# FFN up products with the operand's high and low part side by side: one 512-column matmul for two of 256, pairs of PSUM banks, and TensorE in program order

## The chip, the cores and the metric

The kernel runs on one core of a Trainium2 chip. The metric is the time of one execution on the device, in microseconds, as the median of several runs. A core has five engines with queues of their own: TensorE (matmuls, PE in the profile; its weight loads are PEld), VectorE (DVE), ScalarE (ACT), GpSimd (POOL) and SyncE (SP, which here only issues loads). Matmuls read SBUF and write PSUM, which has eight banks of 512 fp32 columns in each of 128 partitions.

## The reference

One transformer block in fp32 on 512 tokens of width 1024: a gated FFN, a mixer (short convolution and gated linear attention), a second gated FFN, and a last norm.

```python
def swiglu(x, w_gu, w_down):
    g, u = jnp.split(x @ w_gu, 2, axis=-1)
    return (jax.nn.silu(g) * u) @ w_down

def reference(x, ...):
    for l in range(DEPTH):      # DEPTH = 1
        x = x + 0.5 * swiglu(rmsnorm(x, norm_ffn1_g[l]), ffn1_w_gu[l], ffn1_w_down[l])
        x = x + hybrid_mixer(rmsnorm(x, norm_mix_g[l]), ...)
        x = x + 0.5 * swiglu(rmsnorm(x, norm_ffn2_g[l]), ffn2_w_gu[l], ffn2_w_down[l])
    return rmsnorm(x, final_norm_g)
```

The change concerns the "up" products `x @ w_gu` of both FFNs (1024 by 2 x 2816).

## The kernel before, in words

**Precision.** An fp32 product is made from three matmuls in a reduced format (fp32r). Each operand is split into a high part, the rounded value, and a low part, what is left. For a weight these are `wh` (ScalarE, a cast, line 358) and `wl` (VectorE, a subtraction, line 359); for the activations ("op") they are made in `Operands.make` (lines 599 and 600). The product is wh times high + wh times low + wl times high.

**Sets of seven products.** Most of the up projection runs in sets. A set takes 256 columns of the gate g and 256 of u and computes them by a Strassen-like scheme on halves of the depth (1024) and of the tokens (512): seven products instead of eight, called m1, p2, q6, p5, q7, p4, p3, each with another sum of weight blocks and another sum of activation blocks of 256 tokens (HW). There are nine sets in each FFN; the first 512 columns of g and of u run as plain products (`mm_group`, `mm_single`) before them. The order of the products comes from `order`: q6, p5, q7 of set s, m1 of the next set, p4 of s, p2 of the next, p3 of s; so the next set's first products lie between the last ones of this set.

**One product** (`Set.run`) is four pieces of depth k, two halves e of 128 output columns, and three matmuls of 256 tokens each (line 551): 24 matmuls, all into one PSUM bank. The bank is "b" for m1, q6, q7, p4 (which accumulate in it one after the other), "a" for p2, "c" for p5 and p3. After m1, q6 and q7 the state of the bank is kept: ScalarE copies it to SBUF (line 556, tiles "tp"). `done` of `up_set` then makes g1 after p2 (line 715, silu 716), u2 after q7 (line 720), the first half of `hid` after p4 (line 724), g2 after p3 (line 729, silu 730) and the second half of `hid`. In the second FFN, `natural(i)` transposes one block of X (four small matmuls, line 817) after a set.

**Weights** (`Weights`): tiles "f" are loaded by SP, some sums of blocks are made by DMAs that accumulate (line 333, issued by GpSimd) and one by VectorE (line 343). `take` issues the cast and the split of weights two products ahead; `wh` and `wl` have three buffers each, so a cast waits until TensorE has used the buffer of three products before.

**Order.** A scheduler orders each engine's instructions when the program is built, by when they are ready in its own model, and in program order where several are ready; it draws up TensorE's queue as well. In a block of manual schedule an engine keeps program order. At run time every engine works through its queue in that order, and semaphores hold an instruction until what it reads is there and what it overwrites has been read.

**PSUM.** A pool `ps` of six single banks serves all matmuls with tile "mm" (taken in turn), a pool `pa` of two banks the rest ("aux": transposes, sums of squares, two of the down projection's eight banks).

Of the kernel before, what the change touches and what calls it, by code (L numbers as in the profile page):

```python
# [78 lines left out]
HW = 256  # L79
# [136 lines left out]
def block_kernel(ctx: ExitStack, tc: tile.TileContext, xT, vecs, gf, gup, wgl, wts, out):  # L216
    nc = tc.nc
# [2 lines left out]

    front = ctx.enter_context(tc.tile_pool(name="front", bufs=1))
    keep = ctx.enter_context(tc.tile_pool(name="keep", bufs=1))
    ps = ctx.enter_context(tc.tile_pool(name="ps", bufs=6, space=bass.MemoryType.PSUM))
    pa = ctx.enter_context(tc.tile_pool(name="pa", bufs=2, space=bass.MemoryType.PSUM))

    cnt = [0]

# [10 lines left out]
    def tile_of(pool, shape, dtype=F32):  # L238
        cnt[0] += 1
        return pools[pool].tile(shape, dtype, tag=pool, name=f"{pool}{cnt[0]}")  # L240

    def T(dtype=F32):
        return tile_of("tp", [P, S], dtype)

    def MM():
        cnt[0] += 1
        return ps.tile([P, S], F32, tag="mm", name=f"mm{cnt[0]}")

    def AUX():
        cnt[0] += 1  # L250
        return pa.tile([P, S], F32, tag="aux", name=f"aux{cnt[0]}")
# [23 lines left out]
    class Weights:  # L275
# [3 lines left out]
        def __init__(self, ahead):  # L279
            self.ahead = ahead  # L280
            self.issued = 0
            self.taken = 0
            self.end = 0
            self.ready = []
            self.raw = {}
            self.loads = {}
            self.sums = {}
            self.pre = {}
# [88 lines left out]
    W = Weights(2)  # L377
# [12 lines left out]
    def mm_single(mat, kt, col, ah, al):  # L390
        o = MM()
        for u in single(mat, kt, col):
            h, l = W.take(u)
            for i in range(u[2]):
                k = u[1] + i
                mm3(o, h[:, i * P : (i + 1) * P], l[:, i * P : (i + 1) * P],
                    ah[k], al[k], k == 0, k == kt - 1)
        return o

    def mm_group(mat, kt, cols, ah, al, extra=None, slow=False):  # L400
        o = [MM() for _ in cols]
        n = len(cols)
        for u in group(mat, kt, cols, slow):
            h, l = W.take(u)
            for i in range(u[2]):
                k = u[1] + i
                for j, (w, a) in enumerate(((h, ah), (h, al), (l, ah))):
                    for c in range(n):
                        s = (i * n + c) * P
                        nc.tensor.matmul(o[c], w[:, s : s + P], a[k], start=k == 0 and j == 0,  # L410
                                         stop=k == kt - 1 and j == 2)
                if extra is not None:
                    extra(k)
        return o
# [108 lines left out]
    def mul(out_, a, b, eng=None):  # L523
        (eng or nc.vector).tensor_tensor(out=out_, in0=a, in1=b, op=ALU.mult)


    class Set:
# [8 lines left out]

        def run(self, p):
            b = {"m1": "b", "p2": "a", "q6": "b", "p5": "c", "q7": "b", "p4": "b", "p3": "c"}[p]
            fresh = b not in self.bank
            if fresh:  # L540
                self.bank[b] = MM()
            o = self.bank[b]
            bh, bl = self.group.get(p)
            h, l = W.take()
            for k in range(4):
                for e in range(2):
                    s = slice(k * HW + e * P, k * HW + (e + 1) * P)
                    t = slice(k * HW, (k + 1) * HW)
                    to = o[:, e * HW : (e + 1) * HW]
                    for j, (ww, aa) in enumerate(((h, bh), (h, bl), (l, bh))):  # L550
                        nc.tensor.matmul(to, ww[:, s], aa[:, t],  # L551
                                         start=fresh and k == 0 and e == 0 and j == 0,
                                         stop=k == 3 and j == 2, skip_group_check=True)
            if p in self.keep:
                v = T()
                nc.scalar.copy(v, o)  # L556
                self.v[p] = v
            self.done(self, p)

    class Operands:  # L560

        ORDER = ("m1", "p2", "p5", "q6", "q7", "p3", "p4")

        def __init__(self, b):
            self.b = b
            self.parts = {}
            self.sums = set()

# [19 lines left out]
        def make(self, p):  # L590
            if p in self.parts:
                return
            i = self.ORDER.index(p)
            if i > 0:
                self.make(self.ORDER[i - 1])
            v = self.sum(p)
            h, l = (tile_of("op", [P, 1024], F32R) for _ in range(2))
            hv, lv = (t.rearrange("p (k t) -> p k t", t=HW) for t in (h, l))
            nc.scalar.copy(hv, v)  # L599
            nc.vector.tensor_tensor(out=lv, in0=v, in1=hv.bitcast(F32), op=ALU.subtract)  # L600
            self.parts[p] = (h, l)
# [31 lines left out]
    def run_sets(make, ahead=2, hooks={}, tall=None):  # L633


        at = W.taken
        seq = []
        while STEPS[at + len(seq)][1] is not None:
            seq.append(STEPS[at + len(seq)])
        sets = {n: None for n, _ in seq if n not in TALL}  # L640
        number = {n: i for i, n in enumerate(sets)}
        for n, i in number.items():
            sets[n] = make(i)
        for i, (n, p) in enumerate(seq):
# [12 lines left out]
    def ffn(up, down, norm, nxt, plain, at):  # L657
# [7 lines left out]
        o = mm_group(up, KD, (0, DFF, P, DFF + P), xh, xl, extra=finish, slow=nxt is not None)  # L665
# [17 lines left out]
                xn[j, l] = v  # L683
            return xn[j, l]

        xo = Operands(normed)

        def plain_pair(f, g, u):
            s, t = T(), T()
            mul(s, g, row)  # L690
            nc.scalar.activation(s, s, AF.Silu)
            mul(t, u, row)
            mul(hid[:, f], s, t)
# [5 lines left out]
        for f in range(2, plain):  # L699
# [5 lines left out]
                xo.sum("q6")  # L705
            plain_pair(f, g, u)

        def up_set(i):
            h = hid[:, plain + 2 * i : plain + 2 * i + 2]

            def done(s, p):
                bank, v = s.bank, s.v
                if p == "p2":
                    g1 = T()
                    nc.vector.tensor_tensor(out=g1, in0=bank["a"], in1=v["m1"], op=ALU.add)
                    nc.scalar.activation(g1, g1, AF.Silu)
                    s.g1 = g1
                if p == "q7":
                    u2 = T()
                    nc.vector.scalar_tensor_tensor(out=u2, in0=bank["c"], scalar=-1.0, in1=v["q7"],  # L720
                                                   op0=ALU.mult, op1=ALU.subtract)
                    s.u2 = u2
                if p == "p4":
                    nc.vector.scalar_tensor_tensor(
                        out=h[:, :, :HW], in0=pair(bank["b"]), scalar=-1.0, in1=pair(s.g1),
                        op0=ALU.mult, op1=ALU.mult)
                if p == "p3":
                    g2 = T()
                    nc.vector.tensor_tensor(out=g2, in0=bank["c"], in1=v["q6"], op=ALU.add)
                    nc.scalar.activation(g2, g2, AF.Silu)  # L730
                    mul(h[:, :, HW:], pair(s.u2), pair(g2))
                    if nxt is None and i < KD:
                        natural(i)

            return Set(xo, done)

        def pair(t):
            return t.rearrange("p (e t) -> p e t", t=HW)

        run_sets(up_set)  # L740

        def split_hid(k):

# [10 lines left out]
        def banks():  # L754
            return [AUX(), AUX()] + [MM() for _ in range(KD - 2)]
# [12 lines left out]
        o = banks()  # L768
        hls = {k: split_hid(k) for k in (CHUNK, CHUNK + 2)}
        more = [4, 6, 8, 10, "m1", "p2", "p5", "q6", "q7", "p3"]  # L770
        for k in range(CHUNK, KF - TAIL1):
# [3 lines left out]
            if more:  # L775
                n = more.pop(0)
# [25 lines left out]
        o = banks()  # L802
# [702 lines left out]
```

## Time and profile before

| | |
|---|---|
| runs | 1195.34, 1195.03, 1195.0 us; median 1195.03 |
| profiled execution | 1195.04 us, span 1193.3 us |
| mean granted TensorE clock | 0.998 |
| PE, PEld busy | 99%, 91% of the span |
| DVE, ACT, POOL busy | 71%, 50%, 9% |
| HBM | 124.55 MB read, 8.39 MB written |

A busy share is an average over the whole kernel. What a change in one stage is worth is read from the chain of waits: the chain that ended last is followed back from the last instruction, at each step to what released it. A group of instructions is given by line, engine, operation, output and inputs, count, then busy us, mean ns of one, and the idle time before it. In a timeline a row is start us, length us, engine, line and operation; in brackets the idle time before it and who ended it.

### The profile page before, as it was taken

How to read it: one execution, taken by the hardware profiler on the slowest of the kernel's cores; microseconds unless marked ns; L12 is line 12 of the kernel's file. 1: busy time of each engine (PE TensorE's matmuls, PEld its weight loads, DVE VectorE, ACT ScalarE, POOL GpSimd, SP SyncE). 2: the span in 40 equal slices, each digit the busy share in tenths (PEclk: the TensorE clock that was granted, in tenths of full speed). 3: DMA queues.
4: the chain of work that ended last, by engine and by line, in shares of the span. 5: the costliest groups of instructions: out<-in, count | busy, mean ns of one | idle time of the engine just before them, and what ended most of it. 6: DMA issues, size and time to landing. Idle time of an engine off the chain costs nothing.

```text
span 1193.3 us, 19134 instructions
## 1 busy us (share of the span) xinstructions
PE 1183.7 (99%) x7834; PEld 1091.4 (91%) x7834; DVE 841.7 (71%) x1010; ACT 591.7 (50%) x736; POOL 106.4 (9%) x143
## 2 busy tenths in 40 slices
PE   9999999999999999999999999999999999999997
PEld 8899999988988889999999998888889999998886
DVE  7976666854787976667787786555597656675675
ACT  6554454622452746464554574334355555562353
POOL 0011111000110110101111100100001111100100
PEclk9999999999999999999999999999999999999999
DMA  9477777633482767778666766602637777763431
GB/s 345 82 210 183 189 177 190 182 89 90 99 278 72 172 158 208 196 185 212 143 152 147 189 172 214 203 18 78 213 81 211 170 184 173 185 174 117 92 92 70
DMA packets 58471, 190.80 MB, mean 160 GB/s; under 512 B 6576, under 2 KB 10800, under 8 KB 58384
## 3 DMA queue, kind: packets, MB, share of 16 engines
q1 hardware_dynamic: 36912, 124.27, 30.5%
q0 software_dynamic: 16832, 60.83, 27.5%
q10 hardware_dynamic: 4640, 4.49, 1.2%
q8 instruction: 61, 1.00, 0.3%
q14 instruction: 26, 0.21, 0.1%
HBM read 124.55 MB, written 8.39 MB: 111 GB/s over the span
## 4 chain that ended last, share of the span: by engine, by line
PE 97%; DVE 2%; issue 1%; ACT 0%; POOL 0%; DVEq 0%; ACTq 0%; POOLq 0%
PE mm L551 52%; PE mm L410 7%; PE mm L388 6%; PE mm L386 6%; PE mm L387 6%; PE mm L627 3%; PE mm L884 3%; PE mm L834 2%; PE mm L835 2%; PE mm L833 2%; PE aux L1173 1%; DVE wl L359 1%; PE aux L386 1%; PE aux L835 1%; PE aux L388 1%; PE aux L834 1%
## 5 line engine op out<-in xcount | busy, mean ns | idle before, releaser
L551 PE MATMUL mm<-op,wh 128*128 128x256 f32 x3584 | 648.8, 284 | 0.0
L358 ACT CAST wh<-f 128x1024 fp32r<-128x1024 f32 (+1 forms) x325 | 339.4, 1046 | 459.0 <-PE mm L551 221.8
L551 PEld LDWEIGHTS mm<-op,wh 128*128 128x128 f32 x3584 | 559.0, 192 | 1.1
L359 DVE TENSOR_TENSOR wl<-f,wh 128x1024 fp32r<-128x1024 f32 (+1 forms) x325 | 394.8, 1219 | 210.9 <-ACT wh L358 205.9
L551 PE MATMUL mm<-op,wl 128*128 128x256 f32 x1792 | 507.5, 283 | 0.9 <-DVE wl L359 0.9
L551 PEld LDWEIGHTS mm<-op,wl 128*128 128x128 f32 x1792 | 343.3, 192 | 1.6 <-DVE wl L359 1.5
L333 POOL DMA_DIRECT2D f<-f x108 | 93.4, 867 | 932.1 <-DVE wl L359 483.1
L386 PE MATMUL mm<-op,wh 128*128 128x512 f32 x340 | 132.3, 389 | 0.0
L387 PE MATMUL mm<-op,wh 128*128 128x512 f32 x340 | 132.3, 389 | 0.0
L388 PE MATMUL mm<-op,wl 128*128 128x512 f32 x340 | 132.3, 389 | 0.0
L387 PEld LDWEIGHTS mm<-op,wh 128*128 128x128 f32 x340 | 63.8, 188 | 13.3
L388 PEld LDWEIGHTS mm<-op,wl 128*128 128x128 f32 x340 | 63.8, 188 | 13.2
L386 PEld LDWEIGHTS mm<-op,wh 128*128 128x128 f32 x340 | 63.8, 188 | 13.2
L410 PE MATMUL mm<-op,wh 128*128 128x512 f32 x256 | 64.5, 394 | 0.0
L410 PEld LDWEIGHTS mm<-op,wh 128*128 128x128 f32 x256 | 48.6, 190 | 10.4
L556 ACT COPY tp<-mm 128x512 f32<-128x512 f32 x90 | 52.2, 580 | 2.0 <-DVE tp L1323 2.0
L599 ACT CAST op<-hid 128x1024 fp32r<-128x1024 f32 x28 | 29.4, 1051 | 37.4 <-PE aux L834 20.7
L600 DVE TENSOR_TENSOR op<-hid,op 128x1024 fp32r<-128x1024 f32 x28 | 34.2, 1222 | 17.7 <-ACT op L599 17.6
L343 DVE TENSOR_TENSOR f<-f,f 128x1024 f32<-128x1024 f32 x36 | 44.0, 1223 | 0.8
L627 PE MATMUL mm<-wh,op 128*128 128x512 f32 x112 | 34.9, 389 | 0.0
L884 PE MATMUL mm<-wh,op 128*128 128x512 f32 x112 | 34.6, 389 | 0.0
L410 PE MATMUL mm<-op,wl 128*128 128x512 f32 x128 | 34.2, 389 | 0.0
(252 smaller groups left out, 1107.7 us busy)
## 6 DMA issues: line engine op xcount, KB each, us to landing
f<-wts SPq DMA_DIRECT2D x219, 512.0 KB, 4.4
f<-f POOLq DMA_DIRECT2D x108, 512.0 KB, 5.0
X<-xT SPq DMA_DIRECT2D x8, 256.0 KB, 5.3
xs<-X POOLq DMA_DIRECT2D x8, 256.0 KB, 5.5
ga<-tp ACTq DMA_DIRECT2D x8, 256.0 KB, 5.3
gb<-tp ACTq DMA_DIRECT2D x8, 256.0 KB, 5.3
tp<-ga SPq DMA_DIRECT2D x8, 256.0 KB, 5.9
tp<-gb SPq DMA_DIRECT2D x8, 256.0 KB, 3.0
```

The costliest lines, as they stand in the source:

```text
L333: nc.gpsimd.dma_start(out_, a, accum_op=ALU.add)
L343: nc.vector.tensor_tensor(out=s3, in0=a11, in1=a21, op=ALU.add)
L358: nc.scalar.copy(h[:, :w], raw[:, :w])
L359: nc.vector.tensor_tensor(out=l[:, :w], in0=raw[:, :w], in1=h[:, :w].bitcast(F32), op=ALU.subtract)
L386: nc.tensor.matmul(o, wh, ah, start=first, stop=False)
L387: nc.tensor.matmul(o, wh, al, start=False, stop=False)
L388: nc.tensor.matmul(o, wl, ah, start=False, stop=last)
L410: nc.tensor.matmul(o[c], w[:, s : s + P], a[k], start=k == 0 and j == 0, stop=k == kt - 1 and j == 2)
L551: nc.tensor.matmul(to, ww[:, s], aa[:, t], start=fresh and k == 0 and e == 0 and j == 0, stop=k == 3 and j == 2, skip_group_check=True)
L556: nc.scalar.copy(v, o)
L627: nc.tensor.matmul(self.bank[b][e], aa[:, c], ww, start=fresh and i == 0 and n == 0, stop=k == 3 and n == 2, skip_group_check=True)
L884: nc.tensor.matmul(to, aa[:, c], ww, start=fresh and k == 0 and n == 0, stop=k == 3 and n == 2, skip_group_check=True)
```

## The change

For the up sets of both FFNs alone (`Operands(normed, joint=True)`):

- `Operands.make` puts high and low part of 256 tokens side by side: two tiles, each with two pieces of depth, each piece 256 columns high and 256 columns low. A split is two copies and two subtractions of 512 columns instead of one each of 1024.
- `run_joint`: in the six products that use bank "b" or "c", wh is multiplied with 512 columns (high | low) in one matmul, and wl with the 256 columns of the high part. The output is a pair of banks, one for each e: the first 256 columns of a bank hold wh times high ("main"), the last 256 the two small terms ("cross"). p2 keeps its 24 matmuls of 256 columns, in a bank of `pa`.
- What was one reading of a bank becomes two: `whole` copies the cross part (ScalarE) and adds the main part (VectorE), after m1, q6, q7 and p4; u2 and g2 get a second VectorE instruction.
- The pool of six banks becomes, while the sets run, a pool of three pairs over the same banks: it is closed and opened anew before and after the sets of each FFN (`open_banks`), with waits for each tile.
- The sets run in a block of manual schedule for TensorE.

```diff
+    def open_banks(pairs):
+        if "ps" in banks_of:
+            banks_of["stack"].close()
+        banks_of["stack"] = ExitStack()
...
+            tc.tile_pool(name=f"ps{banks_of['n']}", bufs=3 if pairs else 6,
+                         space=bass.MemoryType.PSUM, reuse_waits="tile"))
...
+    def MM2():
+        cnt[0] += 1
+        return banks_of["ps"].tile([P, 2, S], F32, tag="mm", name=f"mm{cnt[0]}")
...
+        def run_joint(self, p, b):
+            fresh = b not in self.bank
+            two_banks = b != "a"
+            if fresh:
+                self.bank[b] = MM2() if two_banks else AUX()
+            o = self.bank[b]
+            parts = self.group.get(p)
+            h, l = W.take()
+            for k in range(4):
+                a = parts[k // 2][:, (k % 2) * S : (k % 2 + 1) * S]
+                for e in range(2):
+                    s = slice(k * HW + e * P, k * HW + (e + 1) * P)
+                    if two_banks:
+                        nc.tensor.matmul(o[:, e], h[:, s], a, start=fresh and k == 0,
+                                         stop=False, skip_group_check=True)
+                        nc.tensor.matmul(o[:, e, HW:], l[:, s], a[:, :HW], start=False,
+                                         stop=k == 3, skip_group_check=True)
+                        continue
+                    to = o[:, e * HW : (e + 1) * HW]
+                    for j, (ww, aa) in enumerate(((h, a[:, :HW]), (h, a[:, HW:]),
+                                                  (l, a[:, :HW]))):
+                        nc.tensor.matmul(to, ww[:, s], aa, start=k == 0 and e == 0 and j == 0,
+                                         stop=k == 3 and j == 2, skip_group_check=True)
+            if p in self.keep:
+                v = T()
+                self.whole(b, v)
+                self.v[p] = v
+            self.done(self, p)
+
+        def whole(self, b, v):
+            o = self.bank[b]
+            v = v.rearrange("p (e t) -> p e t", t=HW)
+            nc.scalar.copy(v, o[:, :, HW:])
+            nc.vector.tensor_tensor(out=v, in0=o[:, :, :HW], in1=v, op=ALU.add)
...
+            if self.joint:
+                t = [tile_of("op", [P, 1024], F32R) for _ in range(2)]
+                for i in range(2):
+                    a = t[i].rearrange("p (k b t) -> p k b t", b=2, t=HW)
+                    vi = v[:, 2 * i : 2 * i + 2]
+                    nc.scalar.copy(a[:, :, 0], vi)
+                    nc.vector.tensor_tensor(out=a[:, :, 1], in0=vi,
+                                            in1=a[:, :, 0].bitcast(F32), op=ALU.subtract)
+                self.parts[p] = t
+                return
...
-        xo = Operands(normed)
+        xo = Operands(normed, joint=True)
...
                 if p == "q7":
...
+                    s.u2 = T()
+                    nc.vector.scalar_tensor_tensor(out=pair(s.u2), in0=main(bank["c"]),
+                                                   scalar=-1.0, in1=pair(v["q7"]),
                                                    op0=ALU.mult, op1=ALU.subtract)
+                    if xo.joint:
+                        nc.vector.tensor_tensor(out=pair(s.u2), in0=pair(s.u2),
+                                                in1=cross(bank["c"]), op=ALU.subtract)
                 if p == "p4":
...
+                    b = pair(bank["b"]) if not xo.joint else pair(v["q7"])
+                    if xo.joint:
+                        s.whole("b", v["q7"])
+                    nc.vector.scalar_tensor_tensor(out=h[:, :, :HW], in0=b, scalar=-1.0,
+                                                   in1=pair(s.g1), op0=ALU.mult, op1=ALU.mult)
                 if p == "p3":
                     g2 = T()
...
+                    nc.vector.tensor_tensor(out=pair(g2), in0=main(bank["c"]), in1=pair(v["q6"]),
+                                            op=ALU.add)
+                    if xo.joint:
+                        nc.vector.tensor_tensor(out=pair(g2), in0=pair(g2), in1=cross(bank["c"]),
+                                                op=ALU.add)
...
-        run_sets(up_set)
+        if xo.joint:
+            open_banks(True)
+        with tc.manual_schedule(engines={ENG.PE}):
+            run_sets(up_set)
+        if xo.joint:
+            open_banks(False)
```

More of the change, by code (lines that the diff above doesn't have):

```diff
@@ L222, in block_kernel @@
     keep = ctx.enter_context(tc.tile_pool(name="keep", bufs=1))
-    ps = ctx.enter_context(tc.tile_pool(name="ps", bufs=6, space=bass.MemoryType.PSUM))
     pa = ctx.enter_context(tc.tile_pool(name="pa", bufs=2, space=bass.MemoryType.PSUM))
+    banks_of = {}
+    def open_banks(pairs):
+        if "ps" in banks_of:
+            banks_of["stack"].close()
+        banks_of["stack"] = ExitStack()
+        banks_of["n"] = banks_of.get("n", 0) + 1
+        banks_of["ps"] = banks_of["stack"].enter_context(
+            tc.tile_pool(name=f"ps{banks_of['n']}", bufs=3 if pairs else 6,
+                         space=bass.MemoryType.PSUM, reuse_waits="tile"))
+    open_banks(False)
+    ctx.callback(lambda: banks_of["stack"].close())
     cnt = [0]
@@ L246, in MM @@
         cnt[0] += 1
-        return ps.tile([P, S], F32, tag="mm", name=f"mm{cnt[0]}")
+        return banks_of["ps"].tile([P, S], F32, tag="mm", name=f"mm{cnt[0]}")
+    def MM2():
+        cnt[0] += 1
+        return banks_of["ps"].tile([P, 2, S], F32, tag="mm", name=f"mm{cnt[0]}")
     def AUX():
@@ L538, in run @@
             b = {"m1": "b", "p2": "a", "q6": "b", "p5": "c", "q7": "b", "p4": "b", "p3": "c"}[p]
+            if self.group.joint:
+                return self.run_joint(p, b)
             fresh = b not in self.bank
@@ L558, in run, with __init__ @@
             self.done(self, p)
+        def run_joint(self, p, b):
[31 more added lines that the diff above has]
+            nc.vector.tensor_tensor(out=v, in0=o[:, :, :HW], in1=v, op=ALU.add)
     class Operands:
         ORDER = ("m1", "p2", "p5", "q6", "q7", "p3", "p4")
-        def __init__(self, b):
+        def __init__(self, b, joint=False):
             self.b = b
+            self.joint = joint
             self.parts = {}
@@ L706, in ffn, with main, cross @@
             plain_pair(f, g, u)
+        def main(t):
+            return t[:, :, :HW] if xo.joint else pair(t)
+        def cross(t):
+            return t[:, :, HW:]
         def up_set(i):
@@ L718, in done @@
                 if p == "q7":
-                    u2 = T()
-                    nc.vector.scalar_tensor_tensor(out=u2, in0=bank["c"], scalar=-1.0, in1=v["q7"],
+                    s.u2 = T()
+                    nc.vector.scalar_tensor_tensor(out=pair(s.u2), in0=main(bank["c"]),
+                                                   scalar=-1.0, in1=pair(v["q7"]),
                                                    op0=ALU.mult, op1=ALU.subtract)
-                    s.u2 = u2
+                    if xo.joint:
+                        nc.vector.tensor_tensor(out=pair(s.u2), in0=pair(s.u2),
+                                                in1=cross(bank["c"]), op=ALU.subtract)
                 if p == "p4":
-                    nc.vector.scalar_tensor_tensor(
-                        out=h[:, :, :HW], in0=pair(bank["b"]), scalar=-1.0, in1=pair(s.g1),
-                        op0=ALU.mult, op1=ALU.mult)
+                    b = pair(bank["b"]) if not xo.joint else pair(v["q7"])
[3 more added lines that the diff above has]
+                                                   in1=pair(s.g1), op0=ALU.mult, op1=ALU.mult)
                 if p == "p3":
                     g2 = T()
-                    nc.vector.tensor_tensor(out=g2, in0=bank["c"], in1=v["q6"], op=ALU.add)
+                    nc.vector.tensor_tensor(out=pair(g2), in0=main(bank["c"]), in1=pair(v["q6"]),
[3 more added lines that the diff above has]
+                                                op=ALU.add)
                     nc.scalar.activation(g2, g2, AF.Silu)
@@ L738, in pair @@
             return t.rearrange("p (e t) -> p e t", t=HW)
-        run_sets(up_set)
+        if xo.joint:
[3 more added lines that the diff above has]
+        if xo.joint:
+            open_banks(False)
         def split_hid(k):
```

## The prediction

> **What bounds the kernel now.** I read the page first (parts 1 and 4), then the chain in order of time, then stretches of time, groups of instructions, and the timelines of the engines inside one set.
>
> ```profile
> span 1193.3 us, 19134 instructions
> PE 1183.7 (99%) x7834; PEld 1091.4 (91%) x7834; DVE 841.7 (71%) x1010; ACT 591.7 (50%) x736; POOL 106.4 (9%) x143
> ...
> PE 97%; DVE 2%; issue 1%; ACT 0%; POOL 0%; DVEq 0%; ACTq 0%; POOLq 0%
> ```
>
> The chain that ended last is TensorE for 97% of the span. So a saving there shortens the kernel, as long as nothing else comes into the chain in its place. The profiled execution took 1195.04 us, 1.7 us beside its span of 1193.3; the median of the runs is 1195.03, so I make the sum against 1195.0. A change of 0.2% is 2.4 us, about what a measurement can tell from none.
>
> Now the chain in order of time (start us, length us, what), for two sets of the second FFN and two stretches of 512-column matmuls:
>
> ```profile
> 843.00 16.33 PE mm L410 x72
> ...
> 913.36 20.16 PE mm L551 x168
> ...
> 933.96 20.16 PE mm L551 x168
> ...
> 1126.34 38.08 PE mm L884 x168
> ```
>
> A set is seven products of 24 matmuls, 168 in 20.16 us without a gap: 120.0 ns for 256 columns, 2.88 us a product. With 512 columns it is 16.33/72 = 226.8 ns and 38.08/168 = 226.7 ns. From 256 to 512 columns the price rises by 106.7 ns, so each matmul carries 13.3 ns that do not depend on its columns.
>
> **The gain.** In six of seven products, h times the high part and h times the low part become one matmul of 512 columns. A product goes from 24 matmuls to 8 of 512 and 8 of 256: 8 x 226.7 + 8 x 120.0 = 2.774 us, 0.107 less. The number of sets is the count of this group:
>
> ```profile
> L715 DVE TENSOR_TENSOR tp<-mm,tp 128x512 f32<-128x512 f32 x18 | 12.4, 691 | 7.6 <-PE mm L551 7.6
> L724 DVE SCALAR_TENSOR_TENSOR hid<-mm,tp 128x512 f32<-128x512 f32 x18 | 12.3, 684 | 0.0
> ...
> L556 ACT COPY tp<-mm 128x512 f32<-128x512 f32 x90 | 52.2, 580 | 2.0 <-DVE tp L1323 2.0
> L600 DVE TENSOR_TENSOR op<-hid,op 128x1024 fp32r<-128x1024 f32 x28 | 34.2, 1222 | 17.7 <-ACT op L599 17.6
> ```
>
> 18 sets x 6 products x 8 pairs = 864 merged pairs, and 864 x 13.3 ns = **11.5 us**. The trace has no alternation of 512 and 256 columns; the bounds are 0 (the 13.3 ns come back in another form) and 11.5, and I take 11.5, because two stretches of 512 and two of 256 give the same remainder.
>
> The Trainium skill (TensorE: Matmul & The Clock Gate, Back-to-back issue gap) gives N/2.4 + 2.5 ns for a warm matmul of N columns; by it a pair would save 2.5 ns and the whole change 2.2 us. The trace disagrees: it has 13.3 where the page has 2.5.
>
> **What the gain costs.** Main part and cross part now lie in two halves of a bank pair and must be joined. Where a set copied one bank on ScalarE (q6, q7, m1), it now copies the cross halves (ScalarE) and then adds the main halves (VectorE); p4 gets both anew; u2 and g2 need a second VectorE instruction each. That is 4 adds + 2 = 6 more VectorE instructions of 0.69 us and one more copy of 0.58 us a set. What matters is where they stand in the queues. One set of the first FFN, ends of q6 and q7 (start us, length us, engine, line, what):
>
> ```profile
> 138.60 1.23 DVE L359 TENSOR_TENSOR wl<-f,wh 128x1024 fp32r<-128x1024 f32 x1 [0.33 <-ACT wh L358]
> 139.75 0.69 DVE L524 TENSOR_TENSOR hid<-tp,tp 128x512 f32<-128x512 f32 x1
> 141.47 1.23 DVE L359 TENSOR_TENSOR wl<-f,wh 128x1024 fp32r<-128x1024 f32 x1 [1.04 <-ACT wh L358]
> ...
> 147.19 1.23 DVE L359 TENSOR_TENSOR wl<-f,wh 128x1024 fp32r<-128x1024 f32 x1 [1.61 <-ACT wh L358]
> 148.33 0.68 DVE L720 SCALAR_TENSOR_TENSOR tp<-mm,tp 128x512 f32<-128x512 f32 x1
> ```
>
> ```profile
> 140.39 1.05 ACT L358 CAST wh<-f 128x1024 fp32r<-128x1024 f32 x1 [1.29 <-issue]
> 141.34 0.58 ACT L556 COPY tp<-mm 128x512 f32<-128x512 f32 x1
> ...
> 146.11 1.05 ACT L358 CAST wh<-f 128x1024 fp32r<-128x1024 f32 x1 [1.79 <-PE mm L551]
> 147.06 0.58 ACT L556 COPY tp<-mm 128x512 f32<-128x512 f32 x1
> ```
>
> ```profile
> 140.15 0.28 PE L551 MATMUL mm<-op,wl 128*128 128x256 f32 x1
> 140.27 0.40 PE L551 MATMUL mm<-op,wh 128*128 128x256 f32 x2
> ...
> 145.91 0.28 PE L551 MATMUL mm<-op,wl 128*128 128x256 f32 x1
> 146.03 0.40 PE L551 MATMUL mm<-op,wh 128*128 128x256 f32 x2
> ```
>
> q6 ends and p5 begins at 140.27; q7 ends and m1 of the next set begins at 146.03. At each end ScalarE casts the next weights first (the last matmul with wh ends before the last with wl) and copies the bank second; VectorE splits wl as soon as the cast is there, and what needs the copy comes behind it: u2 at 148.33, though its copy had ended at 147.64.
>
> q7 accumulates into the bank pair of q6, so its first matmul has to wait for the add of q6. The add stands where u2 stands now. For q6: wl starts at 141.47, the next VectorE instruction 1.15 later (as 138.60 to 139.75), at 142.62, the add ends at 143.31, TensorE goes on some 0.04 later, at 143.35. But p5 is now done at 140.27 + 2.774 = 143.04: TensorE **waits 0.31 us**. For q7, which p4 follows in the same pair with only m1 between: the add runs from 148.33 to 149.02, TensorE could go at 149.06, m1 is done at 146.03 + 2.774 = 148.80: **0.26 us**. Before, only the copy had to be done (141.92), so there was over a microsecond to spare. The other joins (m1, p4, and u2 and g2 for the bank of the next p3 and m1) have three products before their banks are written again and cost nothing unless VectorE lags by over 5 us.
>
> Sum of these waits: 18 x 0.57 = **10.3 us**. Bounds: 0 if the add goes ahead of the split (its copy ahead of the cast), 14 if each wait is 0.1 longer than the rows say. I take 10.3, since u2 shows the order. Behind the waiting matmul stands all of TensorE's queue, and the casts that wait for its weight buffers.
>
> No row shows a matmul that waits for a bank's reader. The Trainium skill (PSUM — Partial Sum Buffer, Terms) says that TensorE writing and VectorE reading one bank at once is an error, so by it the wait can't be left out.
>
> **The first sets.** Two stretches of the second FFN (length, busy time and count of PE, PEld, DVE, ACT, POOL, then clock, DMA): the first set, in which the operands for q6, q7, p3 and p4 are made too, and the second.
>
> ```profile
> 886.80:912.90 26.10, 26.10 (x219) 26.06 (x219) 24.55 (x24) 16.77 (x21) 4.28 (x5) 1.00 0.83 193
> 912.90:933.50 20.60, 20.60 (x175) 20.60 (x174) 12.90 (x13) 10.33 (x14) 2.59 (x3) 1.00 0.75 182
> ```
>
> In a later set VectorE goes from 12.9 to 12.9 + 6 x 0.69 = 17.0 of 20 us: full, not over. In the first it has 24.55 of 26.10 already; 6 x 0.69 and some 0.16 for each of four operands split in halves (2 x 0.69 against 1.22) make 29.3, while seven of the nine products there shorten the stretch to 25.4. The 3.9 us too many need not all show: a wl split is done over 3 us before its product (the one at 141.47 to 142.70 serves m1 at 146.03), so lag costs only where an add is late. Bounds 0 and 3.9 for each FFN; I take 1.5, **3.0** for both.
>
> TensorE in program order: the sets run in it already (168, 168, ...). One place shows another order, q6 of the first FFN:
>
> ```profile
> 50.46 0.40 PE L551 MATMUL mm<-op,wh 128*128 128x256 f32 x2
> ...
> 56.21 0.64 PE L551 MATMUL mm<-op,wh 128*128 128x256 f32 x4
> 57.03 0.39 PE L551 MATMUL mm<-op,wl 128*128 128x256 f32 x1 [0.18 <-DVE wl L359]
> ```
>
> Four wh matmuls before the first wl hide some 0.2 us; that is within what I count for the first sets.
>
> **Banks handed over.** The pairs lie over the six single banks. In the first FFN the eight single-bank tiles before the sets take banks 0 to 3, 4, 5, 0, 1 in turn, so pair 0, for m1, lies on the banks of the last plain product. They are free when VectorE has read them:
>
> ```profile
> 50.59 1.22 DVE L581 SCALAR_TENSOR_TENSOR hid<-hid 128x1024 f32<-128x1024 f32 x1
> 51.73 0.69 DVE L524 TENSOR_TENSOR tp<-mm,row 128x512 f32<-128x512 f32 x1
> ```
>
> m1 can start at 52.5 instead of 50.46, 2.0 us later. VectorE works off its lag meanwhile, which spares first-set waits; bounds 0 and 2.0, I take **0.7**. In the second FFN the count of tiles since the pool was opened puts the last two banks under pair 1, needed three products later: nothing. Behind the sets the first banks wanted are the two of the pool that is left alone, or a pair free since p4 or before: nothing.
>
> p2 keeps its 24 matmuls, in a bank of the other pool, where two are enough, since one is read at once. DMA is unchanged; casts in the sets wait for TensorE, not for loads, so loads that start some tenths later stay hidden.
>
> **Sum:** 1195.0 - 11.5 + 10.3 + 3.0 + 0.7 = **1197.5 us**. Own range of this case: 1192 (waits 0.1 shorter each, first sets 1) to 1203 (0.1 longer, first sets 4).
>
> **Rivals.**
>
> *The add is early.* If copy and add go ahead of cast and split, the add ends at 140.27 + 0.1 + 0.58 + 0.69 = 141.7, over a microsecond before p5 ends; no wait. For it: the order in both queues is drawn up anew. Against: both ends above show the cast first. 1195.0 - 11.5 + 0 to 4 for the first sets: 1184 to 1188, say 1186.
>
> *The hand-over drains (the slower side).* If a newly opened set of banks waits for all old banks, not only for those under it, both openings and both closings stop TensorE. First FFN 2.0 instead of 0.7. Second FFN:
>
> ```profile
> 886.85 0.40 PE L551 MATMUL mm<-op,wh 128*128 128x256 f32 x2
> ...
> 887.84 0.68 DVE L524 TENSOR_TENSOR tp<-mm,row 128x512 f32<-128x512 f32 x1
> ```
>
> 888.52 - 886.85 = 1.7 us; each closing waits for g2's two instructions, 0.2 + 2 x 0.69 = 1.6. In all 1.3 + 1.7 + 3.2 = 6.2 on top: 1203.7. It decides as soon as one wait covers a whole pool. Against: the pools are opened with waits for each tile.
>
> *The merge saves little.* If the 13.3 ns belong to each weight and its columns together, so that a 512 beside a 256 takes nearly two 256, the gain is 0 to 4 and a product lasts some 2.85 us; the waits shrink to 0.23 and 0.18 (7.4 a kernel): 1195.0 - 2 + 7.4 + 3.7 = 1204. This is the case in which the page's 2.5 ns would hold. Against: four stretches of the trace.
>
> **Chances.** Forecast 0.60, early add 0.24, draining hand-over 0.11, little merge 0.05. The forecast's middle lies on the bound of 0.2% (1197.4), so I split it: 0.30 slower, 0.25 same, 0.05 faster. Faster 0.24 + 0.05 = 0.29, same 0.25, slower 0.30 + 0.16 = 0.46. The range of 1185 to 1204 leaves out part of the early add's low end and of the two slower rivals, some 0.15; the forecast's own is 1192 to 1203.
>
> **What would show it.** Instructions: PE 7834 - 864 = 6970, DVE 1010 + 108 + 14 = 1132, ACT 736 + 18 + 14 = 768. If I am right, a set still takes some 20.1 us, 16 matmuls take 2.77 us, and the chain has two pieces of VectorE's add a set, behind the splits of wl. If the add stands ahead of wl, or a set takes 19.5 us, the early add holds. Stops of over 1 us at the four openings and closings are the hand-over's. A product of 2.85 us is the little merge. VectorE filled over 95% in the later sets would mean that I have counted its work too low.

## The result: slower, 1204.2 us

The changed kernel takes 1204.18 us (median; 1203.94 to 1204.6) against 1195.01 us before: 9.2 us more, ratio 1.008, 95% interval 1.0067 to 1.0093. The forecast was 1197.5 us, slower as the likeliest side; the measured time lies 0.2 us above the stated range of 1185 to 1204.

The page of the changed kernel, parts 1 and 4. In the changed file the 512-column matmuls are line 592, those with wl 594, p2's 600, the cast 375, the split of wl 376, the join's copy and add 611 and 612.

```profile
span 1202.5 us, 17553 instructions
PE 1184.7 (99%) x6970; PEld 1043.2 (87%) x6970; DVE 906.6 (75%) x1132; ACT 605.2 (50%) x768; POOL 106.1 (9%) x143
...
PE 89%; DVE 7%; ACT 2%; issue 1%; DMA 1%; DVEq 0%; ACTq 0%
```

The counts are the forecast ones (6970, 1132, 768). PE still reads 99% busy, though its share of the chain fell from 97% to 89%. The busy share hides the waits, because the profile models a matmul's end: at the wait of 0.25 us at 145.72 (rows below) the row before ends at 145.63, so that only 0.09 us look idle. The chain shows the waits. Its 8 points are not lost time, though: they make 96 us, and the loss is 9.2, since TensorE works on beside a cast or a split through which the chain runs. A piece of it in order of time, at the end of q7 and m1 of the set whose queues the prediction drew up:

```profile
148.74 1.06 ACT wh L375
149.80 0.02 issue
149.82 1.23 DVE wl L376
151.04 0.61 DVE tp L612
151.66 0.04 issue
151.70 0.51 PE mm L592
```

This is the wait as forecast: cast, split of wl, add of the join, and only then p4's first matmul. The timelines of VectorE and ScalarE there have the forecast order too, cast before copy and wl before add:

```profile
149.82 1.23 DVE L376 TENSOR_TENSOR wl<-f,wh 128x1024 fp32r<-128x1024 f32 x1 [1.92 <-ACT wh L375]
150.96 0.68 DVE L612 TENSOR_TENSOR tp<-mm,tp 128x512 f32<-128x512 f32 x1
```

```profile
148.74 1.05 ACT L375 CAST wh<-f 128x1024 fp32r<-128x1024 f32 x1 [2.09 <-PE mm L592]
149.69 0.58 ACT L611 COPY tp<-mm 128x512 f32<-128x512 f32 x1
```

What the waits cost in all stands in the groups of TensorE's weight loads (idle before them, who ended it), since the weight load of the first matmul waits with it:

```profile
L592 PEld LDWEIGHTS mm<-op,wh 128*128 128x128 f32 x864 | 162.2, 188 | 54.9 <-DVE tp L612 14.8 <-ACT wh L375 1.8 <-issue 0.8
```

14.8 us were waits for the join, in 30 places. Forecast were 10.3 for the sets and 3.0 for the first sets. So the joins were priced about right, and the loss must also come from the gain. TensorE's timeline, the end of p5 and the start of q7:

```profile
144.41 0.40 PE L592 MATMUL mm<-op,wh 128*128 128x512 f32 x1
144.64 0.28 PE L594 MATMUL mm<-op,wl 128*128 128x256 f32 x1
144.76 0.40 PE L592 MATMUL mm<-op,wh 128*128 128x512 f32 x1
...
145.12 0.40 PE L592 MATMUL mm<-op,wh 128*128 128x512 f32 x1
145.35 0.28 PE L594 MATMUL mm<-op,wl 128*128 128x256 f32 x1
145.72 0.50 PE L592 MATMUL mm<-op,wh 128*128 128x512 f32 x1
146.07 0.28 PE L594 MATMUL mm<-op,wl 128*128 128x256 f32 x1
...
147.24 0.40 PE L592 MATMUL mm<-op,wh 128*128 128x512 f32 x1
...
151.12 0.40 PE L592 MATMUL mm<-op,wh 128*128 128x512 f32 x1
```

From 147.24 to 151.12 eleven pairs take 3.88 us, 0.353 a pair; forecast was 0.2267 + 0.1200 = 0.3467, and three matmuls of 256 took 0.360. Half of the gain is missing here. Counted through the whole timeline, where no wait lies between, 399 pairs of the first FFN take 0.3527 us in the mean and 391 of the second 0.3510. By these means the 864 pairs save 432 x 7.3 + 432 x 9.0 ns = 7.0 us, not 11.5.

At the wait at 145.72, l (the matmul with wl) is followed after 0.37 us instead of 0.12 (0.25 of wait; at p4 it is 0.22), and the first h (with wh) is followed after 0.35 instead of 0.23: a restart costs another 0.11. The weight load that waits is late by both, so the 14.8 us hold the restarts too.

p2's matmuls mark the sets in the chain, in the first FFN and in the second:

```profile
113.76 2.87 PE aux L600 x24
134.27 2.88 PE aux L600 x24
154.79 2.88 PE aux L600 x24
...
934.82 2.88 PE aux L600 x24
955.73 2.88 PE aux L600 x24
```

A set takes 20.51 us (20.16 before) and 20.91 (20.60 before, from 913.36 to 933.96 with its transposes).

The opening of the second FFN's sets, TensorE's timeline:

```profile
891.17 0.39 PE L405 MATMUL mm<-op,wl 128*128 128x512 f32 x1
892.92 0.47 PE L592 MATMUL mm<-op,wh 128*128 128x512 f32 x1 [1.36 <-DVE tp L541]
```

m1 waits for VectorE to read the last plain product (892.09 to 892.77 in VectorE's timeline); with the usual 0.23 us after the last matmul it could have started at 891.40, so 1.52 us are lost. In the first FFN the same gap is 0.52 us, from 49.80:

```profile
50.32 0.47 PE L592 MATMUL mm<-op,wh 128*128 128x512 f32 x1 [0.36 <-DVE tp L541]
```

There m1 goes on after the reading at 49.48 to 50.17, and ahead of the reading of the last plain product, which starts at 51.22.

### The profile page after: what moved, and what is told of

Its sections match the earlier page's. It is cut to its first block, busy times and chain, and to the rows that moved or that the text cites. A ratio compares the mean times of both kernels' runs of the same rounds, so it can differ in the third digit from the quotient of the medians.

```text
span 1202.5 us, 17553 instructions
## 1 busy us (share of the span) xinstructions
PE 1184.7 (99%) x6970; PEld 1043.2 (87%) x6970; DVE 906.6 (75%) x1132; ACT 605.2 (50%) x768; POOL 106.1 (9%) x143
## 4 chain that ended last, share of the span: by engine, by line
PE 89%; DVE 7%; ACT 2%; issue 1%; DMA 1%; DVEq 0%; ACTq 0%
PE mm L570 22%; PE mm L592 15%; PE mm L427 7%; PE mm L594 7%; PE mm L405 6%; PE mm L404 6%; PE mm L403 6%; PE aux L600 4%; PE mm L692 3%; PE mm L969 3%; DVE wl L376 3%; ACT wh L375 2%; PE mm L918 2%; PE mm L920 2%; PE mm L919 2%
## 5 line engine op out<-in xcount | busy, mean ns | idle before, releaser
L592 PE MATMUL mm<-op,wh 128*128 128x512 f32 x864 | 310.8, 402 | 7.3 <-DVE tp L612 3.7
L570 PE MATMUL mm<-op,wh 128*128 128x256 f32 x1568 | 285.0, 284 | 0.0
L570 PEld LDWEIGHTS mm<-op,wh 128*128 128x128 f32 x1568 | 244.9, 192 | 0.9
L594 PE MATMUL mm<-op,wl 128*128 128x256 f32 x864 | 242.5, 281 | 0.4 <-DVE wl L376 0.4
L570 PE MATMUL mm<-op,wl 128*128 128x256 f32 x784 | 222.6, 284 | 0.7 <-DVE wl L376 0.6
L592 PEld LDWEIGHTS mm<-op,wh 128*128 128x128 f32 x864 | 162.2, 188 | 54.9 <-DVE tp L612 14.8
L594 PEld LDWEIGHTS mm<-op,wl 128*128 128x128 f32 x864 | 163.3, 189 | 0.7 <-DVE wl L376 0.7
L570 PEld LDWEIGHTS mm<-op,wl 128*128 128x128 f32 x784 | 150.1, 191 | 1.2 <-DVE wl L376 1.1
L403 PE MATMUL mm<-op,wh 128*128 128x512 f32 x340 | 132.3, 389 | 0.0
L404 PE MATMUL mm<-op,wh 128*128 128x512 f32 x340 | 132.3, 389 | 0.0
L405 PE MATMUL mm<-op,wl 128*128 128x512 f32 x340 | 132.3, 389 | 0.0
L403 PEld LDWEIGHTS mm<-op,wh 128*128 128x128 f32 x340 | 63.8, 188 | 13.3
L404 PEld LDWEIGHTS mm<-op,wh 128*128 128x128 f32 x340 | 63.8, 188 | 13.3
L405 PEld LDWEIGHTS mm<-op,wl 128*128 128x128 f32 x340 | 63.8, 188 | 13.2
L427 PE MATMUL mm<-op,wh 128*128 128x512 f32 x256 | 63.6, 390 | 0.6 <-DVE op L478 0.6
L427 PEld LDWEIGHTS mm<-op,wh 128*128 128x128 f32 x256 | 48.0, 188 | 11.0 <-ACT acc L487 0.8
L600 PE MATMUL aux<-op,wh 128*128 128x256 f32 x288 | 52.6, 283 | 0.0
L612 DVE TENSOR_TENSOR tp<-mm,tp 128x512 f32<-128x512 f32 x72 | 49.4, 687 | 1.8 <-ACT tp L611 0.7
L600 PEld LDWEIGHTS aux<-op,wh 128*128 128x128 f32 x288 | 44.6, 190 | 0.8
```

Source lines behind the costliest of these rows:

```text
L403: nc.tensor.matmul(o, wh, ah, start=first, stop=False)
L404: nc.tensor.matmul(o, wh, al, start=False, stop=False)
L405: nc.tensor.matmul(o, wl, ah, start=False, stop=last)
L570: nc.tensor.matmul(to, ww[:, s], aa[:, t], start=fresh and k == 0 and e == 0 and j == 0, stop=k == 3 and j == 2, skip_group_check=True)
L592: nc.tensor.matmul(o[:, e], h[:, s], a, start=fresh and k == 0, stop=False, skip_group_check=True)
L594: nc.tensor.matmul(o[:, e, HW:], l[:, s], a[:, :HW], start=False, stop=k == 3, skip_group_check=True)
```

## The experiments

**Theory 1:** the joins stand behind the cast and the split of wl, so that q7 and p4 wait in each set; and a pair gains less than was forecast. **Rivals:** the hand-over of the banks; program order on TensorE; the cadence alone. The times are medians, with the ratio to the kernel before measured beside it (whose medians lie between 1194.48 and 1194.79).

**1. TensorE's order left to the scheduler** (a_no_manual)

```diff
-        with tc.manual_schedule(engines={ENG.PE}):
-            run_sets(up_set)
+        run_sets(up_set)
```

> The changed kernel, but the scheduler draws up TensorE's queue in the up sets. Theory 1 (two waits a set for the joins, at q7 and p4, 0.33 us each with the restart, and less gain for each pair): little to put into the gaps, 1201 to 1205 us. Rival (program order costs, since TensorE can't step around what is late): most of the 9 us go, 1194 to 1198 us.

1198.26 us, ratio 1.0031 (1.0020 to 1.0043). Theory 1 expected hardly a change, and was wrong there: 5.9 us of the 9.2 go, nearly what the rival said. TensorE's timeline shows how:

```profile
149.80 0.40 PE L600 MATMUL aux<-op,wh 128*128 128x256 f32 x2
150.03 0.40 PE L592 MATMUL mm<-op,wh 128*128 128x512 f32 x1
...
152.50 0.40 PE L592 MATMUL mm<-op,wh 128*128 128x512 f32 x1
152.73 0.28 PE L594 MATMUL mm<-op,wl 128*128 128x256 f32 x1
152.85 0.29 PE L600 MATMUL aux<-op,wl 128*128 128x256 f32 x1
```

A part of p2, which waits for no bank, is drawn ahead of p4 and fills the time until the add is done. The weight loads' waits for the join fall from 14.8 to 2.6 us:

```profile
PEld mm L592 <- DVE tp L612: 2.6, 4, 1.4
```

Some of that comes back as waits for wl of the p2 that was drawn ahead (the same view lists 3.7 us, 11 times, for its weight loads) and for wl of joint products (2.8 us).

**2. wh last in each product** (b_wh_last)

```diff
+                        last = k == 3 and e == 1
+                        if last:
+                            nc.tensor.matmul(o[:, e, HW:], l[:, s], a[:, :HW], ...)
                         nc.tensor.matmul(o[:, e], h[:, s], a, ...)
+                        if not last:
-                        nc.tensor.matmul(o[:, e, HW:], l[:, s], a[:, :HW], ...)
+                            nc.tensor.matmul(o[:, e, HW:], l[:, s], a[:, :HW], ...)
```

> The changed kernel, but in the last piece of each product the matmul with wl goes first and the one with wh last, so that the bank and the buffer of wh are released together. Theory 1: the copy then stands ahead of the cast and the add ahead of the split of wl, the add ends some 2 us after the product, before the next one is done at 2.8, and the 34 waits of 0.33 us go: 1204.2 - 11 = about 1193 us. If the queues keep the cast first: 1204 us. Rival (the loss is in the cadence of the pairs and the hand-over of banks): 1203 to 1205 us whatever the queues are.

1192.71 us, ratio 0.9985 (0.9975 to 0.9994): 11.5 us less than the changed kernel, as theory 1 had it, and slightly faster than the kernel before. In a joint product of 16 matmuls the last two change places; the work is the same. Both queues turned round. ScalarE, then VectorE:

```profile
145.37 0.58 ACT L616 COPY tp<-mm 128x512 f32<-128x512 f32 x1 [1.72 <-PE mm L596]
145.85 1.05 ACT L375 CAST wh<-f 128x1024 fp32r<-128x1024 f32 x1
```

```profile
145.98 0.69 DVE L617 TENSOR_TENSOR tp<-mm,tp 128x512 f32<-128x512 f32 x1 [1.08 <-ACT tp L616]
146.71 0.69 DVE L796 SCALAR_TENSOR_TENSOR tp<-mm,tp 128x512 f32<-128x512 f32 x1
147.32 1.22 DVE L376 TENSOR_TENSOR wl<-f,wh 128x1024 fp32r<-128x1024 f32 x1
```

The copy goes ahead of the cast, the add starts when the copy is done and ends at 146.67, 1.3 us after the copy's start; wl, which has three microseconds in hand, goes last. The waits for the join are 0.9 us in all now:

```profile
PEld mm L596 <- DVE tp L617: 0.9, 2, 0.6
```

**3. No join** (d_no_join)

```diff
-            nc.scalar.copy(v, o[:, :, HW:])
-            nc.vector.tensor_tensor(out=v, in0=o[:, :, :HW], in1=v, op=ALU.add)
+            nc.scalar.copy(v, o[:, :, :HW])
```

> The changed kernel with the join left out after m1, q6, q7 and p4: ScalarE copies the main half only, no add follows (the small terms of these products are left out of the output). Theory 1: no wait at q7 and p4 and less lag in the first sets, 1204.2 - 12 - 3 = about 1189 us; what is left against before is the gain of the pairs, 5 to 6 us. Rival (cadence and hand-over): 1201 to 1204 us.

1190.76 us, ratio 0.9967 (0.9954 to 0.9979): 13.4 us below the changed kernel. This kernel leaves the small terms of four products out of its output. It gives the ceiling of what the join costs, and it shows what the pairs are worth: only 3.7 us less than the kernel before (1194.48 beside it), with the openings' 2 us still in it. So the pairs gain some 6 us by the times. Its timeline gives a little more: the undisturbed pairs take 0.3531 us in the first FFN and 0.3490 in the second, 7.7 us for 864, while the stages outside the sets are 1.8 us longer in this execution. Either way it is not 11.5.

**4. No bank to wait for at the opening** (f_open_aux)

```diff
-            g = mm_single(up, KD, f * P, xh, xl)
-            u = mm_single(up, KD, DFF + f * P, xh, xl)
+            bank = AUX if f == plain - 1 else MM
+            g = mm_single(up, KD, f * P, xh, xl, bank)
+            u = mm_single(up, KD, DFF + f * P, xh, xl, bank)
```

> The changed kernel with the last plain products (g and u of the fourth column) in the two banks of the other pool, so that no pair lies on a bank that VectorE still has to read when the sets begin. Theory 1: the wait at the opening goes (1.4 us in the second FFN, 0.5 in the first), part of it comes back as lag of VectorE in the first set: 1202.3 to 1203.7 us. Rival (hand-over of banks is the main loss): below 1199 us.

1205.04 us, ratio 1.0088 (1.0073 to 1.0103): no gain at all, outside what theory 1 expected too. The opening waits are gone from TensorE's timeline, but the joins of the first sets come later; the waits of the weight loads, here and (second row) in the changed kernel:

```profile
PEld mm L592 <- DVE tp L612: 17.8, 32, 1.6
```

```profile
PEld mm L592 <- DVE tp L612: 14.8, 30, 1.7
```

3.0 us more for the join in place of 2.0 us at the openings: the wait at the opening was time that VectorE used to catch up. Hand-over as the main loss is refuted.

**5. Program order by itself** (e_before_manual): the kernel before, with `run_sets` inside the block of manual schedule.

> The kernel before, with TensorE in program order in the up sets and nothing else. Theory 1 (program order costs only where a wait stands in TensorE's way, and the sets before have none but 0.2 us): the kernel before within 0.5 us. Rival (program order by itself costs the 6 us that the scheduler's order gave back): 1200 us.

1196.31 us, ratio 1.0012 (1.0002 to 1.0021): 1.5 us, more than the 0.5 us that was expected and far from the rival's 6. TensorE now waits for an operand's low part in the first sets, which it stepped around before:

```profile
PE mm L551 <- DVE op L600: 0.9, 2, 0.5
```

**6. wh last, and TensorE's order left to the scheduler** (i_wh_last_no_manual): experiments 1 and 2 together.

> The changed kernel with wh last in each product, and TensorE's queue drawn up by the scheduler, nothing else. Theory 1: the waits are gone already, so the scheduler's order gives 0 to 2 us on 1192.7 us: 1190.7 to 1192.7. Rival (program order costs 6 us whatever the waits): 1187 us.

1193.78 us, ratio 0.9993 (0.9984 to 1.0002): not faster than with program order (1192.71). It is 1.1 us above what theory 1 expected, and far from the rival's 1187. Without waits at q7 and p4 the scheduler's order has nothing left to fill. So program order cost its 5.9 us in the changed kernel because of the waits.

**7. wh last and no bank to wait for** (g_both): experiments 2 and 4 together.

> The changed kernel with wh last in each product, and the last plain products in the other pool's banks, so that the sets begin at once. Theory 1: the opening waits of 1.7 us go, but VectorE is late in the first sets without them, so at most half of that stays: 1191.5 to 1193 us. Rival (opening waits are a loss of their own): 1190.5 to 1191 us.

1191.72 us, ratio 0.9974 (0.9964 to 0.9985): 1.0 us less than with wh last alone, where the opening was worth nothing in experiment 4. About half of the opening's 2 us stay, as expected; the intervals of the two ratios overlap.

**8. The cadence: h, h, l, l** (c_nojoin_hhll), on the kernel without the join.

```diff
+                    for e in range(2):
+                        nc.tensor.matmul(o[:, e], h[:, ss[e]], a, ...)
+                    for e in range(2):
+                        nc.tensor.matmul(o[:, e, HW:], l[:, ss[e]], a[:, :HW], ...)
```

> The kernel without the join (small terms of m1, q6, q7 and p4 left out of the output), with the order h, h, l, l for the two halves e of each depth in place of h, l, h, l. Theory A (each change from 512 to 256 columns and back costs 6.7 ns): half as many changes, 864 pairs by 3.3 ns, 2 to 3 us less, about 1188 us, two pairs take 0.70 us. Theory B (the 6.7 ns are a state that p2's matmuls leave behind): no difference, 1190.8 us.

1189.00 us, ratio 0.9951 (0.9935 to 0.9968), 1.8 us less than without the join alone, which looks like theory A, though the intervals of the two ratios overlap. By the timelines 2.1 us of it lie in the sets of the first FFN and 0.2 in those of the second, where a fixed price for each change would give the same in both.

**9. The cadence: a small transpose behind p2** (k_nojoin_tick), on the kernel without the join.

```diff
+            if p == "p2":
+                tick = AUX()
+                nc.tensor.transpose(tick[:, :P], ident, ident)
```

> The kernel without the join (small terms left out as before), with one small transpose on TensorE behind each p2, into a bank that nobody reads. Theory B: the pairs behind it take 0.3467 instead of 0.3533 us in the sets of the first FFN, as they do behind the transposes of the second: 9 sets by 48 pairs by 6.7 ns less, 18 transposes by 0.11 us more: about 1190 us, and the cadence shows it in the trace. Theory A: no change of the cadence, 1192.8 us.

1191.50 us, ratio 0.9973 (0.9962 to 0.9984): 0.7 us more, between the two theories. The chain's marks of p2 say more. Without the join (first fence) and with the transpose (second), two sets of the first FFN, then two of the second:

```profile
110.34 2.88 PE aux L600 x24
130.17 2.88 PE aux L600 x24
...
946.36 2.87 PE aux L600 x24
966.37 2.87 PE aux L600 x24
```

```profile
109.43 2.87 PE aux L600 x24
129.06 2.87 PE aux L600 x24
...
944.25 2.87 PE aux L600 x24
964.58 2.88 PE aux L600 x24
```

In the first FFN a set falls from 19.83 to 19.63 us, though a transpose was added; in the second it rises from 20.01 to 20.33, by more than the transpose's own 0.11. Without the join, 48 pairs take 19.83 - 2.88 = 16.95 us in the first FFN, 0.353 each; in the second 20.01 - 2.87 - 0.44 for the transposes = 16.70, 0.348 each. In the first FFN 421 of the 432 pairs now take 0.346 or 0.347 us. So one small matmul moves the cadence of the 40 or more pairs behind it, in the one place down and in the other up. Theory A, a fixed price for each change of width, can't do that.

**10 and 11. Orders with fewer changes of width, joins in place, wh last, no bank to wait for** (m_alt: h, h, l, l and l, l, h, h in turn; o_hhll_wh_last: h, h, l, l three times and l, l, h, h at the end)

> The changed kernel with wh last, the last plain products in the other pool's banks, and the order h, h, l, l and l, l, h, h in turn over the four depths, so that 512 and 256 columns change four times a product. Theory 1 and the cadence: against the same without the new order (1191.7 us) a pair takes 0.348 or less in place of 0.3525 us, 864 pairs by 4 to 6 ns: 1186.5 to 1188.5 us. Rival (the cadence counts only where no join follows): 1191 to 1192 us.

> The changed kernel with the last plain products in the other pool's banks and the order h, h, l, l at the first three depths and l, l, h, h at the last one, so that wh is still last. If the order h, h, l, l gives 0.3483 us a pair (as without the join) and the alternation gave 0.3506: 864 pairs by 2.3 ns less than the alternation's 1190.6 us, about 1188.6 us. If the cadence hangs on what stood before and not on the order: 1190 to 1192 us.

1190.59 us, ratio 0.9967 (0.9955 to 0.9979), and 1190.83 us, ratio 0.9968 (0.9956 to 0.9980): the same within the measurement, 0.9 to 1.1 us below experiment 7, less than the cadence without the join promised: the 1186.5 to 1188.5 us expected of m_alt was missed, and o_hhll_wh_last came out where the cadence does not hang on the order. By the times, the order with fewest changes has no better cadence. m_alt is the fastest version of the study that computes everything, 4.1 us below the kernel before (1194.69 beside it).

**12. m_alt with TensorE's order left to the scheduler** (n_alt_no_manual)

> As the run before, but the scheduler draws up TensorE's queue in the sets. Theory 1 (its order was worth 6 us only because it filled the waits at q7 and p4, which are gone here): within 2 us of the run before. Rival (program order costs by itself): 5 us or more below it.

1191.35 us, ratio 0.9973 (0.9963 to 0.9983): no gain over program order, as in experiment 6.

What sets the cadence between 0.347 and 0.353 us a pair stays open. At 0.347 every pair takes 0.346 or 0.347 us; at 0.353 the pairs take 0.350, 0.349 and 0.361 us in turn (changed kernel, 147.24 to 151.12). Which of the two runs hangs on what TensorE ran before, and no run tells how.

## Why the prediction was wrong, and where it was right

- **The gain, 11.5 us: the step that failed.** The price of a pair was added up from stretches in which all matmuls have one width: 226.7 + 120.0 = 346.7 ns. Side by side the two took 352.7 ns in the mean in the first FFN and 351.0 in the second, so a merged pair saves 8.1 ns in the mean, not 13.3, and all of them 7.0 us. This is 4.5 of the 6.7 us between forecast and measurement. The bound from 0 to 11.5 was named; the value was taken at its upper end. Why a pair costs more beside another width than the sum stays open.
- **The waits at q7 and p4, 10.3 us, and the first sets, 3.0: right in mechanism and nearly in size.** The trace has 14.8 us for both. The waits are 0.25 and 0.22 us instead of 0.31 and 0.26 (the product that covers them is longer by the missing gain), but each restart costs 0.11 us more, which the prediction left out. Experiments 2 and 3 show the mechanism: what takes the add off the path takes 11.5 and 13.4 us off the time.
- **The hand-over, 0.7 us.** 2.0 us at the two openings. For the second FFN the prediction counted tiles and put the last plain product under pair 1; m1 waited for it. For the first it put that product under pair 0; m1 went on ahead of its reading. That experiment 4 gains nothing by removing these waits agrees with the view that they spare first-set waits, which the prediction had for the first FFN.
- **The draining hand-over** (0.11): the openings cost 2.0 us, but at both closings the next matmul starts 0.12 us after the last one of the sets (236.77 and 236.89, 1080.44 and 1080.56), not 1.6 later, and experiment 4 gives nothing back. It did not hold; that its time, 1203.7, came near is luck.
- **The little merge** (0.05): half true. A pair lost two fifths of its gain. Its time, 1204, was the nearest of all, but by luck: it had 2 us of gain where 7.0 were measured, and 10.4 us of waits and 0.7 of hand-over where 14.4 and 2.0 were, and the two errors cancel.
- **TensorE in program order, counted at nothing.** In the kernel before it costs 1.5 us (experiment 5), in the changed one 5.9 (experiment 1). The prediction looked for other orders in the trace of before, where there was little to step around; with a wait put in, the freedom to draw p2 ahead would have been worth two fifths of the waits. The 5.9 us are part of the waits, not a loss beside them.
- **The own range's upper end.** 0.1 us more for each of 36 waits and 4 us for the first sets give 1197.5 + 3.6 + 1.0 = 1202.1, not 1203.
- **Sum.** The spans of the two profiled executions differ by 9.2 us (1193.3 and 1202.5). The sets of both FFNs take 366.9 us before and 374.2 after, 7.3 more; with 7.0 gained by the pairs, the waits in them make 14.4, which agrees with the 14.8 read from the weight loads. The openings are the other 2.0. The rest is -0.2: 0.7 less ahead of the first sets (the last plain product of the first FFN ended at 49.80 us in this execution and at 50.46 in that of before), 0.1 more between the FFNs' sets and 0.4 more behind them. So -7.0 + 14.4 + 2.0 - 0.2 = 9.2, where the forecast had -11.5 + 13.3 + 0.7 = 2.5: the gain is off by 4.5 us, the waits by 1.1, the hand-over by 1.3.

The Trainium skill (TensorE: Matmul & The Clock Gate, Back-to-back issue gap), on which the prediction draws, gives its 2.5 ns for an isolated matmul, and 131 ns at 512 columns for a stream of weight loads and matmuls. Neither is the price here: matmuls of 512 columns with a weight load each took 226.7 ns, and a merged pair saves 6.7 to 13.3 ns. The Trainium skill (PSUM — Partial Sum Buffer, Terms) calls it an error when VectorE reads a bank while TensorE writes it. The chain agrees at p4, whose first matmul starts at 151.70, after the add that ended at 151.65.

## What to carry to other kernels

When a change puts a reading of a bank between two products that accumulate in it, look first at what stands ahead of that reading in the two queues: here it was work with three microseconds to spare, and letting the last matmul release both buffers together turned the order round and was worth 11.5 us. Program order on an engine is cheap while nothing waits (1.5 us in the kernel before), and costs part of the waits once something does (5.9 of 14.4 us here). A matmul's price beside others of another width was not the sum of their prices in pure stretches; take the whole saving as a bound.

## What the runs showed of the hardware that was not expected

- After a wait TensorE restarts slowly: 0.35 us instead of 0.23 until the second matmul (145.72 to 146.07). The weight load had not gone ahead of the wait; weight loads in the changed kernel:

```profile
145.72 0.19 PEld L592 LDWEIGHTS mm<-op,wh 128*128 128x128 f32 x1 [0.41 <-DVE tp L612]
```

- Pairs of 512 and 256 columns run at 0.347 us, or at 0.353 with every third pair 0.011 us longer, and one transpose of 128 columns ahead of them changes which (experiment 9).
- A span that is 99% busy on TensorE by the page had 14.8 us of waits for the join and 2.0 us at the openings in it.
